# The order of the seven products of a 2x2 form: T2 ahead of T1, and the sums of the weights formed earlier

## The chip, the cores and the metric

The kernel runs on one core of a Trainium2 chip. The metric is the device time of one execution in microseconds (us), as the median of several runs. The engines are named as in the profile: PE is TensorE (PEld its weight loads), DVE is VectorE, ACT is ScalarE, POOL is GpSimd, SP is SyncE, which issues most of the DMAs.

## The reference

One layer of a bidirectional encoder, for one sequence of 512 tokens with 1024 features, in float32:

```
h  = rmsnorm(x, g_pre_mix)
q, k, v, g, u, sv, a_ret, a_sgu = split(h @ w_in)        # 512, 512, 1024 x 6 columns
y_ret = (layernorm(retention(q, k, v)) * silu(g)) @ w_ret_o
y_sgu = (gelu(u) * spatial_mix(layernorm(gelu(sv)))) @ w_sgu_o
x1 = x + rmsnorm((sigmoid(a_ret) * y_ret + sigmoid(a_sgu) * y_sgu) @ w_out, g_post_mix)
a, b = split(conv3(rmsnorm(x1, g_pre_ffn) @ w_up))       # 2 x 2816 columns
y  = x1 + rmsnorm((gelu(a) * b) @ w_down, g_post_ffn)
```

The retention runs in chunks of 128 tokens in both directions over 4 heads; the spatial mix is one 128 x 128 matrix for each of 4 groups of channels; conv3 is a depthwise convolution of width 3 over the tokens.

## The kernel before

**The products.** A float32 operand is split into a high half that is rounded to fp32r (`copy` on ACT, L79) and the rest (`tensor_sub` on DVE, L86). A product is then three matmuls: high by high, high by low, low by high (`mm3`, L216 to L219). Activations lie as 128 features by 512 tokens, weights come from HBM in blocks of 128 x 1024 (`wall`), and every weight block is split once, just before it is used.

**The weights' queue.** `units` (L93 to L117) lists all weight blocks in the order of their use. `w_get` (L203) hands out the next one and first issues the work for those that follow, up to 8 or 9 half blocks ahead (`LOOK` is 4): the DMA on SP's queue, the sums and the split. Raw blocks have four buffers (`raw_tile`, L121), split ones nine (`slot`, L126). So the place of a sum or a DMA in the queue of its engine follows from the unit in which it stands. The framework's scheduler then moves some instructions within each engine's order.

**The pairs.** A part of the products is done by a 2 x 2 scheme with seven half products in place of eight: a pair of weight blocks a = B11 | B12 and b = B22 | B21 (512 columns each) and the activations' two halves of tokens and of features. There are 20 pairs: four for u (L741 to L749, profile time 214 to 268 us), four each in the gates of the two branches (`gated_pair`, L784 to L810, 254 to 423 us), and eight couples in the up stage (L1018 to L1029, 520 to 679 us). Seven units feed a pair, in the order of `FORMS` (L92): B11, B21, T1, T2, T3, T4, B22. `w_form` (L156) loads a and b at B11, and forms

- T1 = B11 + B12 and T3 = B12 + B22 on DVE (L167, L168) and T2 = T1 + B22 on POOL (L169), all at the unit T1. T1 and T2 go to a third raw buffer t, T3 takes the place of B12 in a;
- T4 = T2 + B21 on POOL (L171), at the unit T4, in T2's place in t.

Each unit is then split by ACT and DVE into a slot (`wf`).

`Pair.product` (L685, the matmuls at L692) is one such half product: twelve matmuls of 128 x 256 in a row into one of the pair's three PSUM banks. Its argument `first` says whether the bank is begun anew or added onto. `Pair` calls it in three parts:

- `part1` (L704): B11 to bank 0, copied to c0 on ACT (L707); B21 to bank 1, added to c0 on DVE (L709); T1 to bank 2 (L710); T2 added onto bank 0 (L711), copied to c1 on ACT (L712).
- `part2` (L716): T3 added onto bank 0, copied to the second half of c1, and bank 2 minus that on DVE (L720).
- `part3` (L723): T4 added onto bank 0, copied or scaled out (L727 or L729, L730); B22 added onto bank 2, and c1 taken from it (L732).

A product that adds onto a bank waits until the last copy out of that bank has ended. The u pairs run part1, the part3 of the pair before (none for the first), part2; the gates and the couples run part1, an ordinary block of 24 matmuls of 128 x 512 (`f_block`, L665), part2, and a second block with part3 in its middle. c0 and c1 go on to GELU or sigmoid (L730, L735) and, in the up stage, to the convolution (L955, L958, L962) and its gate (L969, L971). For the u stage, `last_turn` (L619) transposes the gated outputs (product at L615, transposes at L624) just ahead of the first pair.

Of the kernel before, what the change touches and what calls it, by code (L numbers as in the profile page):

```python
# [13 lines left out]
ALU = mybir.AluOpType  # L14
# [3 lines left out]
S = 512  # L18
# [29 lines left out]
def tile_block(ctx: ExitStack, tc, xT, x, wall, par, cs, wsp, bsp, gpost, gffn, out):  # L48
    nc = tc.nc
# [6 lines left out]
    def nm(s):  # L56
        uid[0] += 1
        return f"{s}_{uid[0]}"

    def blk(dt=F32, n="blk", shape=(P, S)):  # L60
        return sb.tile(list(shape), dt, tag="blk", bufs=NBLK, name=nm(n))

    def tmp(n="tmp", shape=(P, S)):
        return sb.tile(list(shape), F32, tag="tmp", bufs=6, name=nm(n))
# [13 lines left out]
    def copy(o, i):  # L78
        nc.scalar.activation(out=o, in_=i, func=AF.Copy)  # L79
# [4 lines left out]
    def split(hi, lo, src):  # L84
        copy(hi, src)
        nc.vector.tensor_sub(lo, src, as32(hi))  # L86
# [2 lines left out]

    RES1 = NW - 22 - 44  # L90
    RES0 = RES1 - RES_OUT
    FORMS = ("B11", "B21", "T1", "T2", "T3", "T4", "B22")  # L92
    units = []  # L93
    i = 0
    while i < NW:
        pair = [(f, i) for f in FORMS]
        if U0 <= i < GATE0:
# [5 lines left out]
        elif i == UP0 + 2 * COUPLES[0][0]:  # L103
            for a, b in COUPLES:
                pair = [(f, UP0 + 2 * a) for f in FORMS]
                units += pair[:4] + [("blk", UP0 + 2 * b)] + pair[4:] + [("blk", UP0 + 2 * b + 1)]
# [11 lines left out]
    w_ready, w_pos, w_held, w_raw = {}, [0, 0], [0], {}  # L118

    def raw_tile():  # L120
        return sb.tile([P, 1024], F32, tag="raw", bufs=4, name=nm("raw"))  # L121
# [4 lines left out]
    def slot(n, at=0, w=1024):  # L126
        return sb.tile([P, 1088], F32R, tag="w4", bufs=9, name=nm(n))[:, at : at + w]
# [28 lines left out]
    def w_form(form, i):  # L156

        if form == "B11":
            a, b = raw_tile(), raw_tile()
            nc.sync.dma_start(a, wall[i])  # L160
            nc.sync.dma_start(b, wall[i + 1])
            w_raw["B11"], w_raw["B12"] = a[:, :S], a[:, S:]
            w_raw["B22"], w_raw["B21"] = b[:, :S], b[:, S:]
        elif form == "T1":
            t = raw_tile()
            w_raw["T1"], w_raw["T2"], w_raw["T3"], w_raw["T4"] = t[:, :S], t[:, S:], w_raw["B12"], t[:, S:]
            nc.vector.tensor_add(w_raw["T1"], w_raw["B11"], w_raw["B12"])  # L167
            nc.vector.tensor_add(w_raw["T3"], w_raw["B12"], w_raw["B22"])  # L168
            nc.gpsimd.tensor_tensor(out=w_raw["T2"], in0=w_raw["T1"], in1=w_raw["B22"], op=ALU.add)  # L169
        elif form == "T4":  # L170
            nc.gpsimd.tensor_tensor(out=w_raw["T4"], in0=w_raw["T2"], in1=w_raw["B21"], op=ALU.add)  # L171
        w = slot("wf", 0, 1088)
        lo, hi = w[:, AT_64 : AT_64 + S], w[:, S + AT_192 : 2 * S + AT_192]
        split(hi, lo, w_raw[form])
        return hi, lo
# [21 lines left out]
    def w_unit(u):  # L197
        return w_block(u[1]) if u[0] == "blk" else (w_down if u[0] in "qt" else w_form)(*u)
# [93 lines left out]
    T0, T1 = slice(0, 256), slice(256, 512)  # L292
# [35 lines left out]
    for t in range(NT):  # L328
        for n in range(2):
# [3 lines left out]
                out=xt, in_=xt, func=AF.Square, accum_out=ss[:, 4 * n + t : 4 * n + t + 1]  # L333
# [19 lines left out]
    for c in range(19, 1, -2):  # L353
        v.scalar_tensor_tensor(
            out=lc, in0=lc, scalar=1.0 / c, in1=lb, op0=ALU.add, op1=ALU.mult
# [4 lines left out]
        out=lg, in0=lc, scalar=-2.0, in1=lg, op0=ALU.mult, op1=ALU.add  # L360
# [5 lines left out]
    for m in range(8):  # L366
        t = blk(n="qkraw")
# [286 lines left out]
    for n, acc in enumerate(t_group()):  # L654
        if n < 2:
            for k in (n + 2, n + 6):
                t = tmp("xT")
# [18 lines left out]
    class Pair:  # L676
# [27 lines left out]
        def part1(self):  # L704
            c0, c1 = self.t
            o = self.product(0, self.x(0, T0), True)
            copy(c0[:, T0], o)  # L707
            o = self.product(1, self.x(4, T0), True)
            v.tensor_add(c0[:, T0], o, c0[:, T0])  # L709
            self.product(2, self.s("S1"), True)  # L710
            o = self.product(0, self.s("S2"), False)  # L711
            copy(c1[:, T0], o)  # L712
            if self.scale is not None:
                v.tensor_mul(c0[:, T0], c0[:, T0], self.scale[:, T0])

# [605 lines left out]
```

## Time and profile before

| what | value |
|---|---|
| median of 3 runs | 824.46 us (824.05 to 824.6) |
| the profiled execution | 827.49 us |
| its span from first to last instruction | 825.7 us |
| granted TensorE clock, mean | 0.999 |
| PE busy | 815.4 us (99%) |
| DVE busy | 661.4 us (80%) |
| ACT busy | 440.8 us (53%) |
| POOL busy | 101.0 us (12%) |
| the pairs' matmuls (L692), fp32r high activations by weights, busy | 119.5 us for 640 of them |

How to read the lines that follow: a row of the timeline has the start in us, the duration in us, the engine, the line of the kernel, the operation, output <- inputs by their names in the program, the shapes, and the number of instructions that the row joins. In square brackets stands how long the engine was idle just before it, and whose end released it. A row of the view by stretches has the stretch, its length, then for each engine the busy time and (in brackets) the number of instructions, the granted clock, the share of the DMA engines and GB/s. In the profile POOL's durations are rough.

### The profile page before, as it was taken

How to read it: one execution, taken by the hardware profiler on the slowest of the kernel's cores; microseconds unless marked ns; L12 is line 12 of the kernel's file. 1: busy time of each engine (PE TensorE's matmuls, PEld its weight loads, DVE VectorE, ACT ScalarE, POOL GpSimd, SP SyncE). 2: the span in 40 equal slices, each digit the busy share in tenths (PEclk: the TensorE clock that was granted, in tenths of full speed). 3: DMA queues.
4: the chain of work that ended last, by engine and by line, in shares of the span. 5: the costliest groups of instructions: out<-in, count | busy, mean ns of one | idle time of the engine just before them, and what ended most of it. 6: DMA issues, size and time to landing. Idle time of an engine off the chain costs nothing.

```text
span 825.7 us, 13263 instructions
## 1 busy us (share of the span) xinstructions
PE 815.4 (99%) x5152; PEld 735.0 (89%) x5152; DVE 661.4 (80%) x1101; ACT 440.8 (53%) x771; POOL 101.0 (12%) x102
## 2 busy tenths in 40 slices
PE   9999999999999999999999999999999999999996
PEld 7888888888899999999988898899999998999996
DVE  7489897878797777767765568979899899988967
ACT  6636445546665444444445685556566566544531
POOL 0010000102121111132211211210111200000001
PEclk9999999999999999999999999999999999999999
DMA  8733222212223232222349111322322341233244
GB/s 294 246 116 102 77 77 77 77 52 78 90 102 129 103 102 80 101 101 103 108 166 339 48 55 55 103 102 103 102 103 102 102 154 52 77 115 129 96 147 154
DMA packets 29215, 93.24 MB, mean 113 GB/s; under 512 B 3360, under 2 KB 4000, under 8 KB 29152
## 3 DMA queue, kind: packets, MB, share of 16 engines
q1 hardware_dynamic: 26928, 86.85, 30.2%
q0 software_dynamic: 1360, 4.46, 1.6%
q10 hardware_dynamic: 864, 1.09, 0.4%
q8 instruction: 40, 0.66, 0.3%
q14 instruction: 23, 0.19, 0.1%
HBM read 88.19 MB, written 4.19 MB: 112 GB/s over the span
## 4 chain that ended last, share of the span: by engine, by line
PE 91%; DVE 6%; ACT 1%; issue 1%; DMA 0%; POOL 0%; DVEq 0%; SPq 0%; POOLq 0%; ACTq 0%
PE ps L692 23%; PE ps L217 12%; PE ps L218 12%; PE ps L219 12%; PE ps L1058 8%; PE ps L481 5%; PE ps L480 5%; PE ps L482 5%; PE ps L836 2%; PE ps L837 2%; PE ps L838 2%; PE ps L1074 1%; PE ps L761 1%; DVE fl L86 1%; PE ps L279 1%
## 5 line engine op out<-in xcount | busy, mean ns | idle before, releaser
L86 DVE TENSOR_TENSOR wl<-raw,wh 128x1024 fp32r<-128x1024 f32 (+1 forms) x93 | 109.1, 1182 | 48.9 <-PE ps L692 24.2
L79 ACT ACTIVATE wf<-raw 128x512 fp32r<-128x512 f32 x140 | 85.3, 627 | 102.7 <-PE ps L218 34.0
L86 DVE TENSOR_TENSOR wf<-raw,wf 128x512 fp32r<-128x512 f32 x140 | 111.1, 808 | 23.3 <-ACT wf L79 22.4
L692 PE MATMUL ps<-sh,wf 128*128 128x256 f32 x640 | 119.5, 277 | 0.0
L79 ACT ACTIVATE wh<-raw 128x1024 fp32r<-128x1024 f32 (+2 forms) x95 | 93.3, 993 | 37.4 <-DMA raw<-wall 17.0
L692 PEld LDWEIGHTS ps<-sh,wf 128*128 128x128 f32 x640 | 101.1, 188 | 0.8 <-ACT u L79 0.2
L217 PE MATMUL ps<-h2h,wh 128*128 128x512 f32 (+1 forms) x256 | 92.4, 363 | 0.7 <-ACT h2h L906 0.7
L218 PE MATMUL ps<-h2l,wh 128*128 128x512 f32 (+1 forms) x256 | 92.4, 363 | 0.0
L219 PE MATMUL ps<-h2h,wl 128*128 128x512 f32 (+1 forms) x256 | 92.1, 361 | 0.0
L692 PE MATMUL ps<-sl,wf 128*128 128x256 f32 x320 | 88.8, 278 | 0.0
L480 PE MATMUL ps<-wh,xh 128*128 128x512 f32 x192 | 75.0, 391 | 0.0
L481 PE MATMUL ps<-wl,xh 128*128 128x512 f32 x192 | 74.9, 390 | 0.0
L482 PE MATMUL ps<-wh,xl 128*128 128x512 f32 x192 | 74.8, 390 | 0.0
L169 POOL TENSOR_TENSOR raw<-raw,raw 128x512 f32<-128x512 f32 x20 | 36.2, 1809 | 235.2 <-DVE raw L167 207.8
L1058 PE MATMUL ps<-dl,fh 128*128 128x256 f32 x216 | 60.8, 281 | 0.1
L1058 PE MATMUL ps<-dh,fl 128*128 128x256 f32 x216 | 60.7, 281 | 0.0
L1058 PE MATMUL ps<-dh,fh 128*128 128x256 f32 x216 | 60.7, 281 | 0.0
L692 PEld LDWEIGHTS ps<-sl,wf 128*128 128x128 f32 x320 | 60.0, 188 | 0.6
L219 PEld LDWEIGHTS ps<-h2h,wl 128*128 128x128 f32 x256 | 48.0, 188 | 7.7
L217 PEld LDWEIGHTS ps<-h2h,wh 128*128 128x128 f32 x256 | 47.9, 188 | 7.9 <-ACT h2h L906 1.0
L692 PE MATMUL ps<-xh,wf 128*128 128x256 f32 x288 | 54.2, 278 | 0.0
L218 PEld LDWEIGHTS ps<-h2l,wh 128*128 128x128 f32 x256 | 48.0, 188 | 6.6
(314 smaller groups left out, 2048.9 us busy)
## 6 DMA issues: line engine op xcount, KB each, us to landing
raw<-wall SPq DMA_DIRECT2D x145, 512.0 KB, 3.6
x<-x SPq DMA_DIRECT2D x24, 256.0 KB, 5.9
xT<-xT SPq DMA_DIRECT2D x8, 256.0 KB, 5.4
x<-x POOLq DMA_DIRECT2D x8, 256.0 KB, 2.4
xT<-xT POOLq DMA_DIRECT2D x4, 256.0 KB, 3.6
out<-zg SPq DMA_DIRECT2D x4, 256.0 KB, 2.0
out<-zs ACTq DMA_DIRECT2D x3, 256.0 KB, 3.5
cs<-cs SPq DMA_DIRECT2D x2, 256.0 KB, 4.1
```

What stands on the lines that cost most here:

```text
L79: nc.scalar.activation(out=o, in_=i, func=AF.Copy)
L86: nc.vector.tensor_sub(lo, src, as32(hi))
L169: nc.gpsimd.tensor_tensor(out=w_raw["T2"], in0=w_raw["T1"], in1=w_raw["B22"], op=ALU.add)
L217: nc.tensor.matmul(o, ah, bh, start=start, stop=False)
L218: nc.tensor.matmul(o, ah, bl, start=False, stop=False)
L219: nc.tensor.matmul(o, al, bh, start=False, stop=stop)
L480: nc.tensor.matmul(acc[t], xh[k][:, c], wh[:, f], start=k == 0, stop=False)
L481: nc.tensor.matmul(acc[t], xh[k][:, c], wl[:, f], start=False, stop=False)
L482: nc.tensor.matmul(acc[t], xl[k][:, c], wh[:, f], start=False, stop=k == KD - 1)
L692: nc.tensor.matmul(o, w_[:, c], a_, start=first and k == n == 0, stop=k == 3 and n == 2, skip_group_check=True,)
L836: nc.tensor.matmul(o, ah, bh, start=k == 0, stop=False)
L1058: nc.tensor.matmul(o, a_[:, c], w_[:, f], start=j == t == i == 0, stop=j == DP - 1 and i == 2 and n not in (M2, M3, M4), skip_group_check= ...
```

## The change

The unit T2 is put ahead of T1, and so is its product: part1 is now B11 (bank 0), B21 (bank 1), T2 (onto bank 0), T1 (bank 2). T2's copy into c1 stands between T2 and T1. In `w_form`, the buffer t is taken at B11, where T1's sum on DVE and T2's on POOL are formed too; T3's sum moves to the unit T2; T4's sum on POOL moves from the unit T4 to the unit T1, and T4 is written into B11's place in a and no longer over T2 in t. The number of instructions on each engine is the same.

```diff
-    FORMS = ("B11", "B21", "T1", "T2", "T3", "T4", "B22")
+    FORMS = ("B11", "B21", "T2", "T1", "T3", "T4", "B22")
...
             w_raw["B11"], w_raw["B12"] = a[:, :S], a[:, S:]
             w_raw["B22"], w_raw["B21"] = b[:, :S], b[:, S:]
+            t = raw_tile()
+            w_raw["T1"], w_raw["T2"], w_raw["T3"], w_raw["T4"] = t[:, :S], t[:, S:], w_raw["B12"], w_raw["B11"]
+            nc.vector.tensor_add(w_raw["T1"], w_raw["B11"], w_raw["B12"])
+            nc.gpsimd.tensor_tensor(out=w_raw["T2"], in0=w_raw["T1"], in1=w_raw["B22"], op=ALU.add)
+        elif form == "T2":
+            nc.vector.tensor_add(w_raw["T3"], w_raw["B12"], w_raw["B22"])
         elif form == "T1":
-            t = raw_tile()
-            w_raw["T1"], w_raw["T2"], w_raw["T3"], w_raw["T4"] = t[:, :S], t[:, S:], w_raw["B12"], t[:, S:]
-            nc.vector.tensor_add(w_raw["T1"], w_raw["B11"], w_raw["B12"])
-            nc.vector.tensor_add(w_raw["T3"], w_raw["B12"], w_raw["B22"])
-            nc.gpsimd.tensor_tensor(out=w_raw["T2"], in0=w_raw["T1"], in1=w_raw["B22"], op=ALU.add)
-        elif form == "T4":
             nc.gpsimd.tensor_tensor(out=w_raw["T4"], in0=w_raw["T2"], in1=w_raw["B21"], op=ALU.add)
...
             o = self.product(1, self.x(4, T0), True)
             v.tensor_add(c0[:, T0], o, c0[:, T0])
-            self.product(2, self.s("S1"), True)
             o = self.product(0, self.s("S2"), False)
             copy(c1[:, T0], o)
+            self.product(2, self.s("S1"), True)
```

In the schedule that results, two pairs keep some matmuls of T1 ahead of T2: the first u pair four, the second pair of the retention gate five. The load of the next pair's b now takes its raw buffer when T1's split and T4's sum are done with t, where before it waited for T3's split to be done with a.

## The prediction, made before the changed kernel was run

> **What bounds the kernel now.** I read the page's busy shares first, then the sums by stage, then TensorE's waits, then the queues of ScalarE (ACT), VectorE (DVE) and GpSimd (POOL) around each place that the change touches. The row of the page, and the view of busy time in the stretches of the u pairs, the gated pairs and the up stage:
>
> ```profile
> PE 815.4 (99%) x5152; PEld 735.0 (89%) x5152; DVE 661.4 (80%) x1101; ACT 440.8 (53%) x771; POOL 101.0 (12%) x102
> 216.60:267.90 51.30, 51.28 (x410) 50.09 (x409) 45.49 (x69) 31.52 (x59) 11.72 (x8) 1.00 0.30 104
> 267.90:423.00 155.10, 155.10 (x1017) 141.03 (x1016) 112.89 (x173) 70.42 (x118) 29.50 (x19) 1.00 0.32 110
> 520.00:679.00 159.00, 159.00 (x1022) 143.64 (x1022) 142.73 (x217) 95.47 (x162) 20.58 (x14) 1.00 0.33 113
> ```
>
> TensorE is busy for 51.28 of 51.30, 155.10 of 155.10 and 159.00 of 159.00 us, at full clock. All 20 pairs lie in these stretches. A sooner sum or an earlier weight can therefore save only what a wait still costs there. Busy PE is modelled, so the waits of the weight loads are the finer view. Those of the pairs' line (L692), with ScalarE's rows that they wait for:
>
> ```profile
> 222.28 0.39 ACT L79 ACTIVATE u<-ps 128x256 f32<-128x256 f32 x1 [0.73 <-PE ps L692]
> 222.71 0.19 PEld L692 LDWEIGHTS ps<-sh,wf 128*128 128x128 f32 x1 [0.22 <-ACT u L79]
> 534.24 0.63 ACT L79 ACTIVATE wf<-raw 128x512 fp32r<-128x512 f32 x1 [1.19 <-POOL raw L169]
> 534.78 0.37 ACT L79 ACTIVATE c<-ps 128x256 f32<-128x256 f32 x1
> 535.20 0.19 PEld L692 LDWEIGHTS ps<-h2h,wf 128*128 128x128 f32 x1 [0.39 <-ACT c L79]
> ```
>
> Both waits are on copies out of bank 0. The first is the only place where T3 follows T2 at once: in the first u pair no earlier pair's part3 is there to stand between, and T3 waits 0.22 us for T2's copy into c1. The second is T4 of the first up couple, which waits 0.39 us for T3's copy, itself late because ScalarE stood 1.19 us at a split of a GpSimd sum. A copy that ends at 222.28 + 0.39 = 222.67 lets the load start at 222.71: a hand-over costs 0.04 us.
>
> **The change part by part.** It adds and removes no instruction: as many products, sums, splits, copies and DMAs.
>
> *Gains.* T1 between T2 and T3 covers the 0.22. The sums of a pair come up to two units sooner, so the 1.19 us stand at 534.24 should go and with it the 0.39. Together 0.61 us. No other wait of L692 appears in the list of waits, so this is the ceiling of the gain in the pairs.
>
> *Loss.* T2 adds onto bank 0, and so must wait until B11's copy into c0 has read it. Before, B21 and T1 stood between B11 and T2; now B21 alone does. T2 now starts where T1 started. So I set T1's first load of before against the end of the c0 copy, pair by pair. For the first couple of the up stage:
>
> ```profile
> 520.04 0.28 PE L692 MATMUL ps<-h2h,wf 128*128 128x256 f32 x1
> 522.66 0.19 PEld L692 LDWEIGHTS ps<-sh,wf 128*128 128x128 f32 x1
> 520.74 0.63 ACT L969 ACTIVATE cv<-cv 128x512 f32<-128x512 f32 x1 [2.54 <-DVE cv L962]
> 521.28 1.14 ACT L79 ACTIVATE wf<-raw 128x512 fp32r<-128x512 f32 x2
> 522.32 0.77 ACT L955 ACTIVATE cv<-ps,part 128x512 f32<-128x512 f32 x1
> 522.99 0.62 ACT L79 ACTIVATE wf<-raw 128x512 fp32r<-128x512 f32 x1
> 523.51 0.37 ACT L79 ACTIVATE c<-ps 128x256 f32<-128x256 f32 x1
> ```
>
> Two products stand between 520.0 and 522.7, some 1.36 us each. B11's product is done by 521.5, but its copy stands fourth behind the GELU at L969, which itself waited 2.54 us for VectorE, and ends at 523.51 + 0.37 = 523.88. Before, T2 began a product after 522.66, at 524.02, and was in time by 0.14. Now it wants to start at 522.66 and is late by 1.22. The other places where the copy would come late, each as T1's first load and then the copy (the third and fourth u pair, a gated pair, the couples 3, 5 and 6 counted from 0):
>
> ```profile
> 236.50 0.19 PEld L692 LDWEIGHTS ps<-sh,wf 128*128 128x128 f32 x1
> 236.30 0.37 ACT L79 ACTIVATE u<-ps 128x256 f32<-128x256 f32 x1
> 246.49 0.19 PEld L692 LDWEIGHTS ps<-sh,wf 128*128 128x128 f32 x1
> 246.46 0.37 ACT L79 ACTIVATE u<-ps 128x256 f32<-128x256 f32 x1
> 282.36 0.19 PEld L692 LDWEIGHTS ps<-sh,wf 128*128 128x128 f32 x1
> 282.28 0.36 ACT L79 ACTIVATE sig<-ps 128x256 f32<-128x256 f32 x1
> 584.51 0.19 PEld L692 LDWEIGHTS ps<-sh,wf 128*128 128x128 f32 x1
> 584.68 0.37 ACT L79 ACTIVATE c<-ps 128x256 f32<-128x256 f32 x1
> 625.51 0.19 PEld L692 LDWEIGHTS ps<-sh,wf 128*128 128x128 f32 x1
> 625.68 0.37 ACT L79 ACTIVATE c<-ps 128x256 f32<-128x256 f32 x1
> 646.01 0.19 PEld L692 LDWEIGHTS ps<-sh,wf 128*128 128x128 f32 x1
> 646.89 0.37 ACT L79 ACTIVATE c<-ps 128x256 f32<-128x256 f32 x1
> ```
>
> Late by 0.17, 0.34, 0.28 (here the scheduler leaves five matmuls of T1 ahead of T2, hence 282.36), 0.54, 0.54 and 1.25. With the first couple's 1.22 these are 4.34 us, and seven hand-overs of 0.04 make 4.62. In the other 13 pairs the copy is in time by up to 0.39 us as it stands. The gain must come off and what the sooner sums do to these copies.
>
> *What the sooner sums do.* GpSimd's T4 (L171) now runs straight after T2 (L169). While GpSimd runs, a VectorE operation on SBUF is slowed, and the copies queue behind what it feeds. Around the fourth u pair and ahead of couple 3:
>
> ```profile
> 241.67 1.30 POOL L171 TENSOR_TENSOR raw<-raw,raw 128x512 f32<-128x512 f32 x1 [3.23 <-DVE wf L86]
> 240.90 0.69 DVE L86 TENSOR_TENSOR wf<-raw,wf 128x512 fp32r<-128x512 f32 x1
> 241.84 1.68 DVE L86 TENSOR_TENSOR wf<-raw,wf 128x512 fp32r<-128x512 f32 x1
> 243.00 0.63 ACT L79 ACTIVATE wf<-raw 128x512 fp32r<-128x512 f32 x1 [0.42 <-POOL raw L171]
> 574.55 1.64 POOL L169 TENSOR_TENSOR raw<-raw,raw 128x512 f32<-128x512 f32 x1 [19.45 <-DVE raw L167]
> 575.30 2.28 DVE L86 TENSOR_TENSOR wf<-raw,wf 128x512 fp32r<-128x512 f32 x2
> 577.66 1.30 POOL L171 TENSOR_TENSOR raw<-raw,raw 128x512 f32<-128x512 f32 x1 [1.47 <-DVE wf L86]
> 578.04 2.00 DVE L86 TENSOR_TENSOR wl<-raw,wh 128x1024 fp32r<-128x1024 f32 x1 [0.46 <-PE ps L692]
> 598.54 1.23 DVE L86 TENSOR_TENSOR wl<-raw,wh 128x1024 fp32r<-128x1024 f32 x1 [2.90 <-issue]
> ```
>
> In the u pairs the split took 1.68 instead of 0.69 and ScalarE waited 0.42 for the sum. With both gone the copies at 236.30 and 246.46 come up to 1.0 us sooner, more than the 0.17 and 0.34 wanted, so I put these two at nothing (the ends: 0 and 0.59 with the hand-overs). The gated pair's copy follows splits that the sums do not feed: 0.28 + 0.04 = 0.32 as it stands.
>
> For couple 3 the slow split at 578.04 is 2.00 - 1.23 = 0.77 us longer than the same one at 598.54. If T4 runs from 574.55 + 1.64 = 576.2, it hits a 0.69 split and makes it 1.68 or so: VectorE gets free at 577.6 + 1.0 = 578.6 instead of 577.6, and the 1.23 split ends at 579.8 instead of 580.04. Only 0.2 of the 0.77 is kept. Where T4 falls into VectorE's 0.46 us of idle time, up to 0.46 is. I take 0.28 between these: 0.54 + 0.04 - 0.28 = 0.3 us, for couple 5 too, whose rows are alike (ends 0 and 0.58 each). Couple 6 by the same relief is 1.25 + 0.04 - 0.28 = 1.0; the stalls of couples 3 and 5 put TensorE later by then, while VectorE goes on, so I take 0.8 (ends 0.5 and 1.29). For couple 0 the copy hangs on VectorE's conv at L962 behind 10 us of crowded work; T2's sum and T4's both leave that stretch, but T4's place there lay beside an operation from PSUM. I take 0.9, nearer to the row (ends 0 and 1.26).
>
> The Trainium skill, page "SBUF — State Buffer", section "SBUF: two separate sides", says that VectorE operations with two SBUF inputs and GpSimd's share a port pair as an exclusive lock: who starts first holds it for the whole instruction and the other blocks. By that rule a T4 moved beside a busy VectorE would cost its whole 1.30 there, keep nothing of the 0.77, and couples 3 and 5 would be 0.58 each, 2.57 instead of 2.01 in the sum below. The rows agree in kind, but the split beside L171 lost 0.77 to 0.99, not 1.30, so the sum goes by the rows.
>
> *The sum.* 0.32 + 0.9 + 0.3 + 0.3 + 0.8 = 2.62 of stalls, less 0.61 gained: 2.01 us more. The profiled execution took 827.49 us (span 825.7 and 1.8 around it) and would take 829.5. The median of the runs shown is 824.46, 3.0 below it; the same 2.01 on it gives **826.5 us**, 0.24% more.
>
> *At nothing.* T1's later product frees bank 2 later, but its reader (L720) waits for T3 anyway. The next pair's second load no longer waits for T3's split: SP issues it sooner, into a DMA share of 0.30 to 0.33. GpSimd's last load of xT now stands behind T4 of the first pair, so behind one sum more; what it feeds is used only in the u stage, and if that came late it would show as a wait on xT of at most the 1.3 us of that sum and T2's before it. TensorE waited for no weights in any pair, so T2's split, wanted one product sooner, has cover; if not, it would show as a wait on VectorE's split.
>
> **The rivals.**
>
> *All copies in time.* ScalarE's queue is freed by the sooner sums everywhere, and c0 is never late. For it: the u pairs, and ScalarE's stands of 1.19 at 534.24. Against it: at couple 0 and the gated pair nothing in the queue ahead of the copy hangs on a sum. Then only the gain is left: 824.46 - 0.61 = 823.85, not slower. It decides if the c0 copies of couples 0 and 6 end 1.2 us sooner than now.
>
> *No relief at all.* The lock only changes place, VectorE (142.73 of 159.00 us busy) stays as full, and the copies are as late as recorded: 824.46 + 4.62 - 0.61 = 828.5.
>
> *Only half.* Couple 0's chain shifts enough to be in time, the rest as forecast: 2.01 - 0.9 = 1.1, 825.6.
>
> *GpSimd takes the place of the output gate.* T4 of the second u pair is now released by the split at 214.54, as the gate's product is due:
>
> ```profile
> 214.54 0.69 DVE L86 TENSOR_TENSOR wf<-raw,wf 128x512 fp32r<-128x512 f32 x1
> 215.15 0.69 DVE L615 TENSOR_TENSOR o<-o,g 128x512 f32<-128x512 f32 x1
> 215.89 0.65 PE L624 MATMUL ps<-ident,o 128*128 128x128 f32 x4 [0.28 <-DVE o L615]
> ```
>
> TensorE already waits 0.28 us for that product. If T4 got in ahead of 215.15, it would take about 1.68 and TensorE would stand 1.0 more: 827.5 with the forecast. The product has 0.1 us or so of lead, which speaks against it.
>
> *The change does not do what it says.* T2 and T3 are next to each other in one pair of twenty, so that part alone is worth 0.22 us: 824.2 if nothing else moved.
>
> **How the numbers follow.** Chances: the forecast 0.42, no relief 0.14, the gate 0.07, only half 0.17, all in time (with the last rival, which gives nearly the same) 0.20. The range takes in all of these: from 823.6, a little below the 823.85, to 828.7, a little above the 828.5; I leave out less than 2 in 10. About 0.2% (1.65 us) is what a measurement of this kernel tells from no change. Faster by more than that, 822.8 or less, would need a wait that I do not see: 0.04. Within it fall the all-in-time case, the half case and a quarter of the forecast's, which lies only 0.4 beyond the bound: 0.43. Slower, 826.1 or more: 0.53.
>
> **What would show it.** In the changed kernel's list of TensorE's waits: L692 waiting for ACT at T2 of the couples near 523, 585, 626 and 647 with 0.3 to 0.9 us each and near 282 with 0.3, some 2.6 in all; the 0.22 at 222.71 and the 0.39 at 535.20 gone; GpSimd's two sums of a pair back to back; no 2.0 us split after them at 578. The prediction is wrong if L692 waits under 1 us in all or over 4, if it waits for splits or sums rather than for the copies, or if a later stage, whose instructions are the same, takes another time.

## The result, and the profile of the changed kernel

The changed kernel takes **832.13 us** (median of 4 runs, 829.51 to 833.32) where the kernel before takes 824.25 (823.64 to 824.6): a ratio of 1.0092, 95% interval 1.0066 to 1.0118. It is slower, as forecast, but by 7.9 us and not by 2.0, and outside the range of 823.6 to 828.7. Its own runs lie 3.8 us apart, those of before in the same measurement 1.0. The profiled execution of the changed kernel, 829.51 us, is the shortest of its four.

The page of the changed kernel, the rows that answer to those of before:

```profile
PE 814.2 (98%) x5152; PEld 732.4 (88%) x5152; DVE 662.8 (80%) x1101; ACT 439.0 (53%) x771; POOL 113.3 (14%) x102
L167 POOL TENSOR_TENSOR raw<-raw,raw 128x512 f32<-128x512 f32 x20 | 47.9, 2395 | 273.7 <-DVE raw L166 181.9
```

The counts of instructions are the same. What grew is GpSimd (POOL): 101.0 us became 113.3, nearly all of it in the 20 sums of T2, which now take 2395 ns on average. In the kernel before the same sums took 1809:

```profile
L169 POOL TENSOR_TENSOR raw<-raw,raw 128x512 f32<-128x512 f32 x20 | 36.2, 1809 | 235.2 <-DVE raw L167 207.8
```

The list of TensorE's waits, its rows for the pairs' products (waited for, us in total, times, longest), and then the timeline of the weight loads at all six places:

```profile
PEld ps L692 <- ACT c L79: 4.8, 4, 1.4
PEld ps L692 <- ACT u L79: 0.4, 1, 0.4
PEld ps L692 <- ACT sig L79: 0.3, 1, 0.3
```

```profile
246.06 0.19 PEld L692 LDWEIGHTS ps<-sh,wf 128*128 128x128 f32 x1 [0.39 <-ACT u L79]
282.22 0.19 PEld L692 LDWEIGHTS ps<-sh,wf 128*128 128x128 f32 x1 [0.26 <-ACT sig L79]
523.59 0.19 PEld L692 LDWEIGHTS ps<-sh,wf 128*128 128x128 f32 x1 [0.66 <-ACT c L79]
578.30 0.19 PEld L692 LDWEIGHTS ps<-h2h,wf 128*128 128x128 f32 x1 [1.41 <-ACT c L79]
620.70 0.19 PEld L692 LDWEIGHTS ps<-h2h,wf 128*128 128x128 f32 x1 [1.41 <-ACT c L79]
642.51 0.19 PEld L692 LDWEIGHTS ps<-h2h,wf 128*128 128x128 f32 x1 [1.32 <-ACT c L79]
```

The input's name tells the product. `sh` is a sum of activations, so the first three are T2 waiting for the c0 copy, the loss that was forecast: 1.31 us in all. `h2h` is an activation itself: at 578.30, 620.70 and 642.51 it is T4 that waits, in the couples 2, 4 and 5, for T3's copy into c1. These three are 4.14 us, and no step of the prediction has them. The two waits of before (0.22 at T3 of the first u pair, 0.39 at T4 of couple 0) are gone.

Why is T3's copy late? ScalarE, GpSimd and VectorE of the changed kernel at the first of the three places:

```profile
576.83 1.15 ACT L79 ACTIVATE wf<-raw 128x512 fp32r<-128x512 f32 x2 [3.52 <-POOL raw L167]
577.88 0.36 ACT L79 ACTIVATE c<-ps 128x256 f32<-128x256 f32 x1
```

```profile
573.47 3.32 POOL L167 TENSOR_TENSOR raw<-raw,raw 128x512 f32<-128x512 f32 x1 [19.28 <-ACT fh L79]
```

```profile
573.16 0.68 DVE L86 TENSOR_TENSOR wf<-raw,wf 128x512 fp32r<-128x512 f32 x1
573.76 0.69 DVE L86 TENSOR_TENSOR fl<-gp,fh 128x512 fp32r<-128x512 f32 x1
574.36 0.68 DVE L86 TENSOR_TENSOR wf<-raw,wf 128x512 fp32r<-128x512 f32 x1
574.96 0.68 DVE L169 TENSOR_TENSOR raw<-raw,raw 128x512 f32<-128x512 f32 x1
```

Read from the bottom: VectorE runs four operations on SBUF without a gap, none of them slowed, until 575.64. GpSimd's sum of T2, issued at 573.47 among them, ends only at 576.79, 3.32 us later. ScalarE stands 3.52 us at the split of that sum, and behind it in the queue waits the copy that frees bank 0 for T4. In the kernel before, the copy stood ahead of these splits:

```profile
573.87 0.38 ACT L79 ACTIVATE c<-ps 128x256 f32<-128x256 f32 x1 [1.29 <-PE ps L692]
574.36 0.63 ACT L79 ACTIVATE wf<-raw 128x512 fp32r<-128x512 f32 x1
576.23 0.63 ACT L79 ACTIVATE wf<-raw 128x512 fp32r<-128x512 f32 x1 [1.24 <-POOL raw L169]
```

There ScalarE also stood 1.24 us at T2's sum, but T3's copy was done by then. In the changed kernel's schedule the copy comes behind both splits in every couple that has another after it; in that of before it does so in the couples 0, 1, 3 and 6, and comes ahead of them in the couples 2, 4 and 5, the three that now stall.

A word on the profiled executions: 829.51 us against 827.49 is only 2.0 more, though the waits say more. The down stage, whose instructions are the same, went slower in the profiled execution of before (first fence: before, second: after; one of three groups alike, the number ahead of the second bar is the mean in ns):

```profile
L1058 PE MATMUL ps<-dl,fh 128*128 128x256 f32 x216 | 60.8, 281 | 0.1
```

```profile
L1058 PE MATMUL ps<-dl,fh 128*128 128x256 f32 x216 | 60.0, 278 | 0.1
```

Three such groups make 2.4 us that have nothing to do with the change. The whole down stage, from its first matmul to the start of its last, takes 818.06 - 706.15 = 111.91 us in the trace of before and 819.75 - 710.99 = 108.76 in that of the changed kernel. Of the 14 traces of this case only `copy_behind` has the long one too (111.92); the others lie at 108.8 to 108.9. The granted clock is 1.00 in both, and the profile shows no reason for it. So a single execution can be 3.15 us longer for a cause that the change does not touch, and I compare a stage: the up stage's length, from its first matmul of 128x512 to the next such matmul after the last couple's seven products. It is 681.64 - 498.26 = 183.38 us before and 686.49 - 498.46 = 188.03 after: **4.65 us more**, which is 0.66 + 1.41 + 1.41 + 1.32 of new waits less the 0.39; the remaining 0.24 is not assigned.

### The profile page after: what moved, and what is told of

Same layout as the page of the kernel before. It is cut to its first block, busy times and chain, and to the rows that moved or that the text cites. A ratio compares the mean times of both kernels' runs of the same rounds, so it can differ in the third digit from the quotient of the medians.

```text
span 827.7 us, 13307 instructions
## 1 busy us (share of the span) xinstructions
PE 814.2 (98%) x5152; PEld 732.4 (88%) x5152; DVE 662.8 (80%) x1101; ACT 439.0 (53%) x771; POOL 113.3 (14%) x102
## 4 chain that ended last, share of the span: by engine, by line
PE 81%; DVE 12%; issue 2%; ACT 2%; POOL 1%; DVEq 0%; POOLq 0%; ACTq 0%
PE ps L692 20%; PE ps L217 10%; PE ps L218 10%; PE ps L219 10%; PE ps L1058 8%; PE ps L480 5%; PE ps L481 5%; PE ps L482 5%; PE ps L1074 2%; PE ps L837 2%; PE ps L836 2%; PE ps L838 2%; POOL raw L167 1%; DVE cv L958 1%; DVE fl L86 1%
## 5 line engine op out<-in xcount | busy, mean ns | idle before, releaser
L692 PE MATMUL ps<-sh,wf 128*128 128x256 f32 x640 | 119.7, 277 | 0.7 <-ACT c L79 0.5
L692 PEld LDWEIGHTS ps<-sh,wf 128*128 128x128 f32 x640 | 101.0, 188 | 2.1 <-ACT c L79 0.7
L692 PE MATMUL ps<-sl,wf 128*128 128x256 f32 x320 | 88.8, 278 | 0.0
L167 POOL TENSOR_TENSOR raw<-raw,raw 128x512 f32<-128x512 f32 x20 | 47.9, 2395 | 273.7 <-DVE raw L166 181.9
L692 PEld LDWEIGHTS ps<-sl,wf 128*128 128x128 f32 x320 | 60.0, 188 | 0.6
L692 PE MATMUL ps<-xh,wf 128*128 128x256 f32 x288 | 53.8, 278 | 0.0
```

The costliest lines, as they stand in the source:

```text
L692: nc.tensor.matmul(o, w_[:, c], a_, start=first and k == n == 0, stop=k == 3 and n == 2, skip_group_check=True,)
```

## The experiments

The theory (A): the loss is mostly T4's wait for T3's copy, which stands on ScalarE behind the split of a GpSimd sum that VectorE holds up. The rival (B): the late c0 copy, which the prediction named, carries it. All runs are in the table, with the length of the up stage in their traces. Each median stands beside that of the kernel before on the same chip.

| run | median us | before | ratio, 95% interval | up stage us |
|---|---|---|---|---|
| the kernel before | | | | 183.38 |
| the changed kernel | 832.13 | 824.25 | 1.0092 (1.0066 to 1.0118) | 188.03 |
| again (the same) | 831.52 | 824.45 | 1.0078 (1.0060 to 1.0097) | 191.36 |
| products_only | 828.86 | 824.14 | 1.0060 (1.0048 to 1.0072) | 186.21 |
| sums_only | 828.12 | 824.14 | 1.0055 (1.0040 to 1.0071) | 188.24 |
| t2_on_vector | 824.23 | 824.14 | 1.0009 (0.9998 to 1.0019) | 183.03 |
| copy_first | 827.45 | 824.14 | 1.0049 (1.0033 to 1.0066) | 184.90 |
| copy_behind | 824.43 | 824.45 | 1.0002 (0.9992 to 1.0012) | 183.35 |
| t4_sum_late | 830.73 | 824.45 | 1.0089 (1.0068 to 1.0111) | 188.03 |
| before_t2_vector | 824.76 | 824.45 | 1.0006 (0.9997 to 1.0015) | 183.03 |
| products_t2_vector | 826.25 | 823.74 | 1.0021 (1.0010 to 1.0032) | 184.03 |
| after_all_vector | 824.29 | 823.74 | 1.0000 (0.9989 to 1.0011) | 183.26 |
| before_all_vector | 823.93 | 823.74 | 0.9995 (0.9983 to 1.0007) | 183.04 |
| first_couple_vector | 829.23 | 823.75 | 1.0072 (1.0052 to 1.0091) | 187.16 |

### The two halves of the change, each alone

`products_only` keeps the units, sums and splits of the kernel before and swaps the products:

```diff
-            self.product(2, self.s("S1"), True)
-            o = self.product(0, self.s("S2"), False)
+            t1, t2 = w_get(), w_get()
+            o = self.product(0, self.s("S2"), False, t2)
             copy(c1[:, T0], o)
+            self.product(2, self.s("S1"), True, t1)
```

> Only the order of the two products is changed: T2 before T1, while units, sums and splits keep the order of the kernel before. Theory A (the loss of the changed kernel is mostly T4 waiting for T3's copy, which now stands behind the split of a GpSimd sum in ScalarE's queue, in the couples 2, 4 and 5): T3's copy keeps its place in ScalarE's queue, so no T4 wait over 0.5 us; what is left is the late c0 copy, 1.3 to 4.3 us by the rows of before, 825.6 to 828.5. Theory B (the late c0 copy carries the loss): nearly the whole loss of the changed kernel, 829.5 or more.

Measured 828.86, 4.7 us more than before and 0.36 above A's range, under B's. T4 waits nowhere. Four of the waits at T2 (weight loads, timeline):

```profile
283.42 0.19 PEld L692 LDWEIGHTS ps<-sh,wf 128*128 128x128 f32 x1 [0.26 <-ACT sig L79]
525.05 0.19 PEld L692 LDWEIGHTS ps<-sh,wf 128*128 128x128 f32 x1 [0.90 <-ACT c L79]
587.16 0.19 PEld L692 LDWEIGHTS ps<-sh,wf 128*128 128x128 f32 x1 [0.52 <-ACT c L79]
650.09 0.19 PEld L692 LDWEIGHTS ps<-sh,wf 128*128 128x128 f32 x1 [0.59 <-ACT c L79]
```

Couple 5 (628.90) waits 0.52 as well. These are the places that the prediction read from the rows of before, with 0.28, 1.22, 0.54 and 1.25 for the four shown: the same sizes or less, the last one least, since TensorE is late there already. So rival B is a real loss by itself: 2.8 us in the up stage, 0.48 us of waits in the u and the gated pairs; the rest of the 4.7 is not assigned. But it is not the loss of the changed kernel, which waits at T2 for c0 in only one of the four couples 0, 3, 5 and 6.

`sums_only` keeps the products' order and forms the sums sooner:

```diff
         if form == "B11":
...
+            t = raw_tile()
+            w_raw["T1"], w_raw["T2"], w_raw["T3"], w_raw["T4"] = t[:, :S], t[:, S:], w_raw["B12"], w_raw["B11"]
+            nc.vector.tensor_add(w_raw["T1"], w_raw["B11"], w_raw["B12"])
+            nc.gpsimd.tensor_tensor(out=w_raw["T2"], in0=w_raw["T1"], in1=w_raw["B22"], op=ALU.add)
         elif form == "T1":
...
             nc.vector.tensor_add(w_raw["T3"], w_raw["B12"], w_raw["B22"])
-            nc.gpsimd.tensor_tensor(out=w_raw["T2"], in0=w_raw["T1"], in1=w_raw["B22"], op=ALU.add)
-        elif form == "T4":
+        elif form == "T2":
             nc.gpsimd.tensor_tensor(out=w_raw["T4"], in0=w_raw["T2"], in1=w_raw["B21"], op=ALU.add)
```

> Only the sums come sooner: T1 and T2 at unit B11, T3 at unit T1, T4 at unit T2 and into B11's place; products and splits keep their order. Theory A: the order of ScalarE's queue that results has T3's copy behind T2's split in every couple, as in the changed kernel, so T4 waits 1 us or more in three couples, 827 to 829. Theory B: T2 still has two products after B11 and c0 is never late, so 824 to 824.5 and no such wait.

Measured 828.12, 4.0 more, as A has it. T2 in couple 0, then T4 and ScalarE in couple 2:

```profile
524.92 0.19 PEld L692 LDWEIGHTS ps<-sh,wf 128*128 128x128 f32 x1 [0.72 <-ACT c L79]
578.28 0.19 PEld L692 LDWEIGHTS ps<-h2h,wf 128*128 128x128 f32 x1 [1.49 <-ACT c L79]
577.33 0.63 ACT L79 ACTIVATE wf<-raw 128x512 fp32r<-128x512 f32 x1 [3.46 <-POOL raw L167]
577.86 0.36 ACT L79 ACTIVATE c<-ps 128x256 f32<-128x256 f32 x1
```

The same stall without the new order of the products. Forming the sums sooner is enough to bring it. B's time of 824 is excluded. Its premise fails too: c0 is late in couple 0 although two products stand between B11 and T2, and GpSimd's sum of T2 takes 5.83 us there (at 507.38). So the sooner sums alone can make a c0 copy late.

### Which part of the stall's chain is needed

`t2_on_vector` is the changed kernel with T2's sum on VectorE:

```diff
-            nc.gpsimd.tensor_tensor(out=w_raw["T2"], in0=w_raw["T1"], in1=w_raw["B22"], op=ALU.add)
+            nc.vector.tensor_add(w_raw["T2"], w_raw["T1"], w_raw["B22"])
```

> The changed kernel with T2's sum on VectorE in place of GpSimd. Theory A: T2's split no longer waits 3 us for GpSimd, and T3's copy stands ahead of it again in the couples 2, 4 and 5; the T4 waits go, the c0 waits stay: 825.5 to 827. Theory B: the c0 copies are as late as before or later, since VectorE has 20 sums of 0.7 us more: 829 or more.

Measured 824.23 against 824.14: the whole loss is gone, more than A had asked for. No product of a pair in the up stage waits over 0.15 us, at T2 or at T4. The 20 sums of 0.7 us cost VectorE nothing that shows. But the schedule also puts T3's copy ahead of the splits again in the couples 2, 4 and 5, so two things changed at once. The next two separate them.

`copy_first` is the changed kernel with GpSimd's sums, and T2's split queued behind T3's copy in the up stage. For that the edit also shortens the look-ahead at two calls of `w_get` (7 and 9 half blocks), so that T2's unit is begun later:

```diff
-    def w_get(look=LOOK):
+    def w_get(look=LOOK, most=None):
...
-        while w_pos[1] < len(units) and (w_pos[1] <= i or n + w_size(units[w_pos[1]]) <= max(room, 9 if look == LOOK else 0)):
+        room = most or max(room, 9 if look == LOOK else 0)
+        while w_pos[1] < len(units) and (w_pos[1] <= i or n + w_size(units[w_pos[1]]) <= room):
...
-        split(hi, lo, w_raw[form])
+        with tc.issue_after(last_c.pop()) if last_c and form == "T2" else ExitStack():
+            copy(hi, w_raw[form])
+        nc.vector.tensor_sub(lo, w_raw[form], as32(hi))
...
-            o = self.product(0, self.s("S3"), False)
-            copy(c1[:, T1], o)
+            o = self.product(0, self.s("S3"), False, w_get(most=None if self.scale is not None else 7))
+            i = nc.scalar.activation(out=c1[:, T1], in_=o, func=AF.Copy)
+            if self.scale is None:
+                last_c[:] = [i.ins]
...
-            o = [f_block(h2h, h2l, KD)]
+            o = [f_block(h2h, h2l, KD, None, 9)]
```

> The changed kernel, but in the up stage the split of T2 is queued on ScalarE behind T3's copy of the couple before (and its unit is begun that much later); sums stay on GpSimd. Theory A: the T4 waits of 1.4 us in the couples 2, 4 and 5 go, c0 waits near 523 and in the gates stay: 825 to 827. Theory B: c0 waits unchanged and so the time, 829.5 to 833. A third, that GpSimd's longer sums starve the products of weights: L692 waits for splits, and the time stays or grows.

Measured 827.45, and the up stage 184.90, 3.1 us shorter than the changed kernel's. That is 0.45 us above A's range. The T4 waits are gone; GpSimd's sums of T2 are as long as without this edit (2445 ns on average, against 2395). The c0 wait of couple 0 is the changed kernel's; one that the prediction had named, in couple 3, now appears:

```profile
523.61 0.19 PEld L695 LDWEIGHTS ps<-sh,wf 128*128 128x128 f32 x1 [0.66 <-ACT c L79]
585.42 0.19 PEld L695 LDWEIGHTS ps<-sh,wf 128*128 128x128 f32 x1 [0.21 <-ACT c L79]
```

Couples 5 and 6 wait 0.21 and 0.16, and the fourth u pair waits 0.81 at 246.60. That the changed kernel has no such waits in the couples 3, 5 and 6 fits its stalls ahead of them, which make TensorE late while ScalarE catches up; no run shows this by itself.

`copy_behind` is `t2_on_vector` with T3's copy forced behind the splits, as in the changed kernel:

```diff
-        split(hi, lo, w_raw[form])
+        i = nc.scalar.activation(out=hi, in_=w_raw[form], func=AF.Copy)
+        if form == "T1":
+            t1_split[:] = [i.ins]
+        nc.vector.tensor_sub(lo, w_raw[form], as32(hi))
...
-            copy(c1[:, T1], o)
+            with tc.issue_after(t1_split[0]) if self.scale is None else ExitStack():
+                copy(c1[:, T1], o)
```

> The kernel with T2's sum on VectorE, but T3's copy is queued on ScalarE behind the next couple's T2 and T1 splits, as the schedule of the changed kernel has it in every couple. If the place in the queue alone costs the 1.4 us: T4 waits over 1 us in the couples 2, 4 and 5, 827 to 829. If it takes GpSimd's long sum as well: the two splits wait for nothing and T3's copy comes 1.1 us later at most, T4 waits under 0.3 us, 824 to 825.

Measured 824.43 against 824.45, and no T4 wait over 0.15 us; the up stage is 0.3 us longer than in `t2_on_vector`. ScalarE in couple 2:

```profile
573.60 1.15 ACT L174 ACTIVATE wf<-raw 128x512 fp32r<-128x512 f32 x2 [1.84 <-DVE raw L167]
574.66 0.36 ACT L79 ACTIVATE c<-ps 128x256 f32<-128x256 f32 x1
```

The splits still wait, 1.84 us for VectorE's sum, but end soon enough. So the stall needs both: the copy behind the split, and a sum of GpSimd that takes 3.3 us. Take away either one and it is gone.

`t4_sum_late` moves T4's sum alone back to the unit T4:

```diff
-        elif form == "T1":
+        elif form == "T4":
             nc.gpsimd.tensor_tensor(out=w_raw["T4"], in0=w_raw["T2"], in1=w_raw["B21"], op=ALU.add)
```

> The changed kernel with T4's sum at the unit T4, as before the change, in B11's place. If T2's long sum ahead of T3's copy carries the loss: the T4 waits of the couples 2, 4 and 5 stay, 828.5 to 832. If it is T4's sum straight behind T2's that holds the port and drags ScalarE's queue: they go or halve, 826 to 828.

Measured 830.73, the up stage 188.03 as in the changed kernel, T4's first wait 1.41 us at 578.39. The place of T4's sum makes no difference to these waits; the prediction had hung its relief on it.

### Why the changed kernel's runs lie 3 us apart

`again` is the changed kernel once more.

> The changed kernel once more, for a second trace and the spread of its times. If the waits of T4 in the couples 2, 4 and 5 are set by the order of the queues, they are there again with 1.3 to 1.5 us each; what differs between a short and a long execution should show as a wait at another place, or as a longer one there.

The three T4 waits are the same (1.41, 1.41, 1.32). The difference of the two traces is at couple 0. GpSimd's sum of T2 there and a VectorE operation beside it, in the first trace of the changed kernel; then the same in `again`, with the end of VectorE's stream, ScalarE's stand and T2's wait:

```profile
507.19 1.67 POOL L167 TENSOR_TENSOR raw<-raw,raw 128x512 f32<-128x512 f32 x1 [23.64 <-DVE raw L166]
507.62 1.78 DVE L971 TENSOR_TENSOR gp<-cv,cv 128x512 f32<-128x512 f32 x1
```

```profile
507.18 5.83 POOL L167 TENSOR_TENSOR raw<-raw,raw 128x512 f32<-128x512 f32 x1 [23.63 <-DVE raw L166]
507.56 0.68 DVE L971 TENSOR_TENSOR gp<-cv,cv 128x512 f32<-128x512 f32 x1
511.18 0.68 DVE L1012 TENSOR_TENSOR h<-h,xs 128x512 f32<-128x512 f32 x1
514.74 0.69 DVE L86 TENSOR_TENSOR sl<-xs,sh 128x512 fp32r<-128x512 f32 x1 [2.88 <-ACT sh L79]
513.03 1.16 ACT L79 ACTIVATE wf<-raw 128x512 fp32r<-128x512 f32 x2 [6.36 <-POOL raw L167]
525.22 0.29 PEld L692 LDWEIGHTS ps<-sh,wf 128*128 128x128 f32 x1 [2.60 <-ACT c L79]
```

The same sum starts at the same time. Once it runs at once and VectorE's operation beside it takes 1.78 us; once VectorE keeps its pace (0.68) and the sum takes 5.83: VectorE's stream ends at 511.86, the sum 1.15 us later. ScalarE then stands 6.36 us, VectorE in turn 2.88 us for ScalarE's splits, and T2 waits 2.60 us for c0 and not 0.66. The up stage is 191.36 us, 3.3 longer.

The longer wait is 1.94 of these 3.3 us. Most of the rest is a slower TensorE right behind it. The view by stretches, first the changed kernel's first trace, then `again`:

```profile
525.20:528.40 3.20, 3.20 (x21) 2.85 (x20) 3.20 (x7) 1.42 (x3) 0.00 (x0) 1.00 0.51 161
525.20:528.40 3.20, 3.18 (x15) 3.18 (x16) 3.20 (x6) 1.71 (x3) 0.00 (x0) 0.50 0.84 279
```

The granted clock is 0.50 there and was 1.00, and single matmuls of 128x256 take 0.41 to 0.42 us where they took 0.28. T4's first wait comes 3.04 us later than in the first trace (581.34 against 578.30), though T2's load was only 1.63 us later (525.22 against 523.59): 1.4 us are lost without a wait. The waits of 1.3 to 1.5 us show no such drop. This is one trace, so that the 2.6 us of idle time caused the drop is likely but not shown.

At 832.73 us this execution is near the median of the changed kernel. So the 7.9 us are told by both traces: 4.14 us of T4's waits in each, and at couple 0 either 0.66 us or 2.60 with the slower clock behind it.

`first_couple_vector` is the changed kernel with that one sum on VectorE:

```diff
-            nc.gpsimd.tensor_tensor(out=w_raw["T2"], in0=w_raw["T1"], in1=w_raw["B22"], op=ALU.add)
+            on = nc.vector if i == UP0 + 2 * COUPLES[0][0] else nc.gpsimd
+            on.tensor_tensor(out=w_raw["T2"], in0=w_raw["T1"], in1=w_raw["B22"], op=ALU.add)
```

> The changed kernel with T2's sum of the first up couple alone on VectorE. If the 3 us between its executions come from that one sum (1.67 us in one trace, 5.83 in the other, with T2 waiting 0.66 or 2.60 for c0 in couple 0): c0 is in time or late by under 0.7 there, the T4 waits of 1.3 to 1.4 in the couples 2, 4 and 5 stay, and the runs lie within about 1 us of 829. If the spread comes from elsewhere: runs from 829 to 833 as before.

Measured 829.23; T2 in couple 0 no longer waits, the T4 waits stay (1.42, 1.41, 1.32). Four of the six runs lie between 828.62 and 829.25, two at 830.91 and 831.84. The up stage, 187.16 us, is the changed kernel's 188.03 less the wait in couple 0. So this sum makes most of the distance from 829 to 832, but not all of the spread; what the other two runs waited for is open. Two candidates are in the traces: T4's sum, still on GpSimd, takes 6.43 us at 511.07 in this very run, without a stall, and the down stage can be 3.15 us longer, as in the trace of before.

### The order of the products without GpSimd, and the sums on VectorE

`products_t2_vector` is `products_only` with T2's sum on VectorE (the edit of `t2_on_vector`).

> Only the order of the products changed, as in the run products only, and T2's sum on VectorE. If the late c0 copies of the up stage come from ScalarE standing at GpSimd's sums: the waits at T2 in the couples 0, 3, 5 and 6 (0.5 to 0.9 us each there) fall under 0.2, the 0.26 near 282 stays, 824 to 825.5. If they come from the order of the products alone: they stay, 828 or more.

Measured 826.25 against 823.74. The waits at T2 fall to 0.16 and 0.17 in the couples 3 and 5, and the up stage's excess from 2.83 to 0.65 us. So most of the late c0 copies too come from GpSimd's sums of T2; whether by ScalarE's stands at them or by the VectorE operations that they slow, this run does not separate. The time is 0.8 above what was expected and 2.5 above before: 0.65 in the up stage and 0.26 in the gated pair (the 0.23 of the first u pair is there before too); the rest is not assigned.

`after_all_vector` and `before_all_vector` have T4's sum on VectorE as well:

```diff
-            nc.gpsimd.tensor_tensor(out=w_raw["T4"], in0=w_raw["T2"], in1=w_raw["B21"], op=ALU.add)
+            nc.vector.tensor_add(w_raw["T4"], w_raw["T2"], w_raw["B21"])
```

> The changed kernel with T2's and T4's sums on VectorE, none on GpSimd. VectorE loses the slowed operations (about 1 us each) and gains 40 sums of 0.7 us. By the theory that GpSimd's sums cause the loss: no waits of L692 in the up stage, 823.5 to 824.5. If VectorE becomes the bound: waits for its splits or copies, 825 or more.

> The kernel before with T2's and T4's sums on VectorE. The 0.39 us of T4 in the first couple goes, the 0.22 of the first u pair stays: 823.7 to 824.5. TensorE is busy nearly all the time, so no more than 0.6 us can come off in the pairs. If VectorE becomes the bound: 825 or more.

Measured 824.29 and 823.93 against 823.74. `before_t2_vector` has T2's sum alone on VectorE, in the kernel before.

> The kernel before with T2's sum on VectorE and nothing else. The wait of T4 in the first couple (0.39 us) goes with GpSimd's sum, the 0.22 of the first u pair stays; VectorE has 20 sums of 0.7 us more, which cost nothing if its splits have lead: 823.5 to 824.5, not to be told from before. If VectorE is the bound somewhere, 825 or more with waits of TensorE for splits.

Measured 824.76 against 824.45, 0.26 above the range expected. In all three no pair's product in the up stage waits over 0.15 us, and its length is 183.03 to 183.26. None can be told from the kernel before: in the pairs there were only 0.6 us of waits to win. No version was found that is faster than the kernel before.

## Why the prediction was wrong

- **What bounds the kernel**: right. The gain in the pairs is bounded by 0.61 us; the three versions of the changed kernel without the stalls (`t2_on_vector`, `copy_behind`, `after_all_vector`) came back to the time of before.
- **The gains**: right in the rows. Both waits are gone, 0.22 and 0.39 (in `products_only` and `after_all_vector` the schedule puts eight matmuls of T1 ahead of T2 in the first u pair, only four are left between T2 and T3, and the 0.22 is back). The reason given for the second was wrong: "the 1.19 us stand at 534.24 should go". ScalarE's stands at T2's sums grew, to 3.52 and 6.36 us. At couple 0, 3.55 us are in place of the 1.19, but that stand ends at 532.81 and not at 534.24, early enough for T4.
- **The loss at c0**: the mechanism was right, and `products_only` shows nearly the sizes that the rows of before gave. In the changed kernel's first trace it is 1.31 us and not 2.62: 0.39 in the fourth u pair (forecast nothing), 0.26 in the gated pair (0.32), 0.66 in couple 0 (0.9; 2.60 in `again`, beyond its upper end of 1.26), and nothing in the couples 3, 5 and 6 (0.3, 0.3, 0.8). The prediction's own sign is met: L692 waits 5.45 us in all, where over 4 was to show it wrong.
- **The step that failed** is "What the sooner sums do". It priced a GpSimd sum by its usual duration, 1.3 to 1.65 us, and asked only what it does to VectorE. It did not ask what VectorE does to the sum. Moved to where VectorE runs four or more operations on SBUF in a row, the sum waits for them: 3.32 us in three couples, up to 5.83 in the first. (Four other sums of 2.7 us in the up stage and four of 3.06 in the gated pairs make no wait of T4.) A row of before's trace had already shown it, the sum of 3.42 us at 510.93 that the working did not use:

```profile
510.93 3.42 POOL L169 TENSOR_TENSOR raw<-raw,raw 128x512 f32<-128x512 f32 x1 [27.27 <-DVE raw L167]
```

- The same step looked only at the c0 copy's place in ScalarE's queue. T3's copy had moved too, behind the splits of the next couple, and of T4 the prediction said only that its one wait would go. That is 4.14 us, shown by `sums_only` (it comes with the sums alone), by `copy_first` (it goes with the place) and by `copy_behind` and `t2_on_vector` (it goes with the sum). The rest of the median's 7.9 us is couple 0, where the same long sum delays c0: 2.60 us and a slower clock in `again`.
- **Luck**: the prediction gave the profiled execution 829.5 us, and it took 829.51. Two errors cancel there: the stalls cost more than forecast, and the 827.49 that it started from held 3.15 us of a slow down stage.
- **The rivals**: "No relief at all" gave 828.5 and so came nearest, but not by its mechanism: the first trace has 1.31 us of c0 waits and not its 4.62, and a stall that it does not name. GpSimd did not take the place of the output gate: TensorE's wait for L615 at the transposes is 0.59 us on the weight loads in both kernels.

## What to carry to other kernels

When a sum on a second engine is moved, look at what the first engine runs at its new place: here the sum took as long as the first engine's whole stream of operations on the same memory, and the queue of the engine that reads the sum passed that wait to everything behind the reader. Compare the order of every copy that frees a bank, not only of those that the edit touches. Where the bounding engine is busy all the time, a reordering can win only the waits that it still has, and lose much more.

## What the runs showed of the hardware

- GpSimd's sums and VectorE's operations with two inputs in SBUF hold each other up in these traces, and which one waits is open between executions of the same program: 1.67 us for the sum and 1.78 for VectorE's operation beside it, or 5.83 for the sum and 0.68 for the operations. The Trainium skill, page "SBUF — State Buffer", section "SBUF: two separate sides", describes an exclusive lock, held for the whole instruction by whoever starts first, with the other fully blocked. The traces agree that one waits for the other, and show more: GpSimd waited for VectorE's stream to break (at 575.64 and 511.86, the sums ending 1.15 us later), and not for one instruction of it.
- The prediction weighed the same rule and used it only for VectorE's loss. Read in both directions, it speaks for a longer sum, though one operation of 0.7 us ahead of a sum of 1.3 makes 2.0 us, an estimate, and not the 3.3 measured.
- In `again` the granted clock of TensorE was 0.50 for 3.2 us right after a wait of 2.60 us; after waits of 1.3 to 1.5 us it stayed at 1.00.
- Moving 40 sums of GpSimd to VectorE did not make the kernel slower than can be told (823.93 against 823.74, ratio 0.9995, interval 0.9983 to 1.0007), though VectorE was 80% busy (81% with them): each sum takes 0.7 us there, and operations that GpSimd's sums had slowed (1.78 us at 507.62 in the changed kernel) take 0.7 beside none. That this is why it costs nothing is argued.
